# Three of the eight pieces of six modulation parts computed on GpSimd instead of VectorE in a two-block transformer kernel

## The chip, the core and the metric

The kernel runs on one core of one Trainium2 chip. The core has engines with a queue each: TensorE (PE in the profile; its weight loads are PEld), VectorE (DVE), ScalarE (ACT), GpSimd (POOL) and SyncE (SP), which here only issues DMAs. Every queue is worked through in order, so an instruction that waits holds up all that stand behind it on its engine. The time is the device time of one launch in microseconds. Before the change it was 1309.55 us (median of three runs, 1307.87 to 1313.42).

## What is computed

Two blocks of two layers each over 256 tokens of width 1024, all in float32. The change lies in the first block, in the vectors that scale, shift and gate each of its layers:

```python
cs = jax.nn.silu(c)
for layer in range(DEPTH):
    mod = cs @ ada_w[layer] + ada_b[layer]
    shift, scale, gate = jnp.split(mod, 3, axis=-1)
    h = rms_norm(x, norm_g[layer]) * (1.0 + scale[:, None, :]) + shift[:, None, :]
    ...
    y = even_mixer(...)      # layer 0; odd_mixer(...) in layer 1
    x = x + gate[:, None, :] * y
```

`cs` is one row of 1024 numbers and `ada_w[layer]` is 1024 x 3072, so the product is a matrix times a vector: little arithmetic for many bytes (25 MB for both layers).

## The kernel before

**The modulation.** A layer's 3072 results are cut into three parts (0 shift, 1 scale, 2 gate) of two halves of 512 columns. For one half of a part the 1024 rows of weights come as eight pieces of 128 x 512 (`k` = 0 to 7), 256 KB each. VectorE multiplies piece `k` by the column `cs[:, k]` and sums the pieces in an accumulator `macc` (`add_k`, L457: a TENSOR_SCALAR for the first piece at L462, a SCALAR_TENSOR_TENSOR at L464 for the others). GpSimd adds the row of `ada_b` into the accumulator's first partition (L519). One matmul with a matrix of ones (L523) then sums over the partitions and spreads the result over all of them, and `finish` (L466) puts it where the layer reads it. Shift and scale of layer 0 are made at the start of the kernel by another function (`start`). The other eight halves are *later parts*: `part` (L511) starts one each time that the function `later` (L889) is called, and `later` first finishes the one before. They are numbered 0 to 7 here in the order of the list `todo`: gate of layer 0 (0, 1), scale of layer 1 (2, 3), shift of layer 1 (4, 5), gate of layer 1 (6, 7).

**What runs beside them.** The later parts are spread over the attention of layer 0 (`even_layer`). Its projections stream weights through `unit` (L220 to L230): SyncE loads `wr` (L224, three buffers), ScalarE rounds it to `wh` (L227), VectorE makes the remainder `wl` (L228; five buffers each), and TensorE does three products for each pair (L245 to L247). Attention of a first kind (heads `scores_a`, `values_a`) has its row minimum with bias on VectorE (L398), the exponential on ScalarE (L401), the scaling by the row's sum on VectorE (L678), then transposes on TensorE (L410); a second kind (`scores_b`, `values_b`) has L398, L401 and L731 in these places, and a GpSimd power (L337) before L751. The results are gated (L592, L579) and go through the output projection with the weights `ab_w_out`.

**What sets the order.** The pieces `aw` have three buffers, and their loads (L517) share SyncE's queue with the weight loads (L224) and the bias tables (L416). A framework schedules the program at build time: it interleaves the instructions of each engine by priorities and by its own estimate of times, and the result is a fixed order per engine. So a change in one place can give another order on all engines. The accumulators `macc` have two buffers.

## Time and profile before

| | |
|---|---|
| time, median of three runs | 1309.55 us |
| the profiled execution: time | 1304.1 us |
| the profiled execution: span of the trace | 1302.3 us |
| TensorE / VectorE / ScalarE / GpSimd busy | 95% / 65% / 49% / 5% of the span |
| the later parts' accumulation | 56.6 to 183.5 us of the span |

The page of the profile gives the busy time of each engine over the span. A view by stretches gives the same for chosen pieces of time; a view by lines groups the instructions by line and form and says what ended the idle time ahead of them; the view of waits says which engine waited for which instruction; the timeline lists instructions with start and length. On GpSimd and VectorE an instruction's length runs from its start to its end, so time in which it is held up after its start counts in its length. Neighbouring VectorE instructions overlap by a little: a SCALAR_TENSOR_TENSOR of 0.75 us starts 0.67 us after the one before.

### The profile page before, as it was taken

How to read it: one execution, taken by the hardware profiler on the slowest of the kernel's cores; microseconds unless marked ns; L12 is line 12 of the kernel's file. 1: busy time of each engine (PE TensorE's matmuls, PEld its weight loads, DVE VectorE, ACT ScalarE, POOL GpSimd, SP SyncE). 2: the span in 40 equal slices, each digit the busy share in tenths (PEclk: the TensorE clock that was granted, in tenths of full speed). 3: DMA queues.
4: the chain of work that ended last, by engine and by line, in shares of the span. 5: the costliest groups of instructions: out<-in, count | busy, mean ns of one | idle time of the engine just before them, and what ended most of it. 6: DMA issues, size and time to landing. Idle time of an engine off the chain costs nothing.

```text
span 1302.3 us, 21332 instructions
## 1 busy us (share of the span) xinstructions
PE 1240.6 (95%) x8352; PEld 1047.7 (80%) x8352; DVE 851.2 (65%) x1456; ACT 644.0 (49%) x1083; POOL 68.9 (5%) x82
## 2 busy tenths in 40 slices
PE   6889889999899999999999999999999999999997
PEld 3767667977787777887899987987787887999986
DVE  6977888676658755766755544668755757655543
ACT  3454645685655345444644433556345444544432
POOL 0021120000101000000000000010000000000000
PEclk8999999999999999999999999999999999999999
DMA  8988865654553233465666654753242564766552
GB/s 315 325 274 277 257 197 172 202 179 122 178 170 98 84 114 98 149 210 162 196 186 185 181 192 129 234 149 96 82 128 83 177 196 130 226 183 188 180 192 81
DMA packets 104960, 227.25 MB, mean 175 GB/s; under 512 B 8206, under 2 KB 8350, under 8 KB 104860
## 3 DMA queue, kind: packets, MB, share of 16 engines
q1 hardware_dynamic: 102560, 219.18, 54.0%
q0 software_dynamic: 1984, 6.60, 1.8%
q8 instruction: 65, 1.06, 0.3%
q14 instruction: 35, 0.29, 0.1%
q10 hardware_dynamic: 316, 0.12, 0.0%
HBM read 224.82 MB, written 1.05 MB: 173 GB/s over the span
## 4 chain that ended last, share of the span: by engine, by line
PE 70%; DVE 7%; issue 5%; ACT 3%; DMA 2%; POOL 1%; POOLq 0%; DVEq 0%; ACTq 0%; SPq 0%
PE mm L246 20%; PE mm L245 19%; PE mm L247 19%; PE p L369 2%; DVE wl L228 2%; PE hs L1156 1%; ACT wh L227 1%; PE sc L376 1%; PE px L1440 1%; PE tr L324 1%; DMA wr<-in_gu_dram 1%; PE pv L385 1%; PE cm L376 1%; PE pt L410 1%; PE pv L1002 1%
## 5 line engine op out<-in xcount | busy, mean ns | idle before, releaser
L228 DVE TENSOR_TENSOR wl<-wr,wh 128x1024 fp32r<-128x1024 f32 (+1 forms) x372 | 431.3, 1165 | 268.6 <-ACT wh L227 266.5
L227 ACT CAST wh<-wr 128x1024 fp32r<-128x1024 f32 (+1 forms) x372 | 369.7, 1002 | 396.7 <-PE mm L247 164.7
L245 PE MATMUL mm<-hh,wh 128*128 128x256 f32 x1168 | 332.1, 286 | 1.0 <-ACT hh L328 0.9
L247 PE MATMUL mm<-hh,wl 128*128 128x256 f32 x1168 | 332.7, 285 | 0.0
L246 PE MATMUL mm<-hl,wh 128*128 128x256 f32 x1168 | 332.3, 285 | 0.0
L245 PEld LDWEIGHTS mm<-hh,wh 128*128 128x128 f32 x1168 | 224.4, 193 | 3.7 <-ACT hh L328 1.9
L247 PEld LDWEIGHTS mm<-hh,wl 128*128 128x128 f32 x1168 | 224.5, 192 | 2.1 <-issue 1.9
L246 PEld LDWEIGHTS mm<-hl,wh 128*128 128x128 f32 x1168 | 224.6, 192 | 1.5 <-issue 1.2
L246 PE MATMUL mm<-wl,hh 128*128 128x512 f32 (+1 forms) x448 | 178.3, 398 | 1.5 <-DVE wl L228 1.5
L245 PE MATMUL mm<-wh,hh 128*128 128x512 f32 (+1 forms) x448 | 177.3, 396 | 0.9 <-DVE ropet L1069 0.4
L247 PE MATMUL mm<-wh,hl 128*128 128x512 f32 (+1 forms) x448 | 175.5, 392 | 0.4 <-DVE hl L329 0.3
L246 PEld LDWEIGHTS mm<-wl,hh 128*128 128x128 f32 x448 | 85.0, 190 | 19.7 <-DVE wl L228 2.4
L245 PEld LDWEIGHTS mm<-wh,hh 128*128 128x128 f32 x448 | 84.9, 190 | 18.7 <-ACT hh L328 1.2
L247 PEld LDWEIGHTS mm<-wh,hl 128*128 128x128 f32 x448 | 84.8, 189 | 17.0 <-DVE hl L329 1.4
L245 PE MATMUL mm<-wh,ff 128*128 128x512 f32 x176 | 69.5, 395 | 0.0
L246 PE MATMUL mm<-wl,ff 128*128 128x512 f32 x176 | 69.5, 395 | 0.0
L247 PE MATMUL mm<-wh,ff 128*128 128x512 f32 x176 | 69.4, 395 | 0.0
L464 DVE SCALAR_TENSOR_TENSOR macc<-aw,cs,macc 128x512 f32<-128x512 f32 x78 | 58.4, 762 | 11.9 <-DMA aw<-in_ada_w_dram 11.5
L401 ACT ACTIVATE p<-p,nm 128x256 f32<-128x256 f32 (+1 forms) x80 | 39.7, 497 | 32.0 <-DVE nm L398 29.2
L246 PE MATMUL mm<-wl,yTh 128*128 128x512 f32 x128 | 50.6, 396 | 1.1 <-DVE wl L228 1.1
L247 PE MATMUL mm<-wh,yTl 128*128 128x512 f32 x128 | 50.0, 390 | 0.0
L245 PE MATMUL mm<-wh,yTh 128*128 128x512 f32 x128 | 49.4, 395 | 0.1
(388 smaller groups left out, 1533.7 us busy)
## 6 DMA issues: line engine op xcount, KB each, us to landing
wr<-in_w_in_dram SPq DMA_DIRECT2D x120, 512.0 KB, 3.8
wr<-in_gu_dram SPq DMA_DIRECT2D x88, 512.0 KB, 3.7
wr<-in_w_ffn_down_dram SPq DMA_DIRECT2D x44, 512.0 KB, 3.3
aw<-in_ada_w_dram SPq DMA_DIRECT2D x80, 256.0 KB, 3.9
wr<-in_ab_w_in_dram SPq DMA_DIRECT2D x32, 512.0 KB, 5.3
wr<-in_c_w_in_dram SPq DMA_DIRECT2D x20, 512.0 KB, 4.4
wr<-in_w_branch_dram SPq DMA_DIRECT2D x16, 512.0 KB, 3.2
wr<-in_w_out_dram SPq DMA_DIRECT2D x16, 512.0 KB, 3.2
```

Source lines behind the costliest of these rows:

```text
L227: nc.scalar.copy(hi[:, i:i + m], raw[:, i:i + m])
L228: nc.vector.tensor_sub(lo[:, i:i + m], raw[:, i:i + m], hi[:, i:i + m].bitcast(F32))
L245: mm(out, lhsT=ah, rhs=bh, start=start, stop=False, **kw)
L246: mm(out, lhsT=ah, rhs=bl, start=False, stop=False, **kw)
L247: mm(out, lhsT=al, rhs=bh, start=False, stop=stop, **kw)
L324: nc.tensor.transpose(ps[:, j * 128:(j + 1) * 128], src[:, (g + j) * 128:(g + j + 1) * 128], self.ident)
L369: self.nc.tensor.matmul(out[r], lhsT=lhsT[:, r], rhs=rhs, **kw)
L376: mm = lambda out, lhsT, rhs: self.nc.tensor.matmul(out, lhsT=lhsT, rhs=rhs, start=True, stop=True)
L385: mm = lambda hh, kc: self.nc.tensor.matmul(ps[HALF[hh], :], lhsT=vs(hh, kc), rhs=pTs[hh][:, kc * 256:kc * 256 + 256], start=(kc == 0), st ...
L401: nc.scalar.activation(p, p, AF.Exp, bias=nm, scale=-1.0, accum_out=l)
L410: nc.tensor.transpose(ps[:, kc * 256 + t * 128:kc * 256 + t * 128 + 128], p[:, t, kc * 128:kc * 128 + 128], self.ident)
L464: nc.vector.scalar_tensor_tensor(acc, w, n.cs[:, k:k + 1], acc, op0=OP.mult, op1=OP.add)
```

## The change

```diff
     def part(self, part, half):
         n, nc = self.n, self.n.nc
         acc = n.s2("macc", tag="macc")
-        for k in range(8):
-            w = n.s2("aw", tag="aw")
-            nc.sync.dma_start(w, self.src(part, half, k, 1))
-            self.add_k(acc, k, w, k == 0)
-        nc.gpsimd.tensor_add(acc[0:1, :], acc[0:1, :], self.row(part, half))
+        if self.l == 0 or part != 2:
+
+            acc2 = n.s2("macc2", tag="macc")
+            for k in (0, 1, 3, 2, 4, 6, 5, 7):
+                w = n.s2("aw", tag="aw")
+                nc.sync.dma_start(w, self.src(part, half, k, 1))
+                if k in (0, 3, 6):
+                    nc.gpsimd.tensor_scalar(w if k else acc2, w, n.cs[:, k:k + 1], None, op0=OP.mult)
+                    if k:
+                        nc.gpsimd.tensor_add(acc2, acc2, w)
+                else:
+                    self.add_k(acc, k, w, k == 1)
+            nc.gpsimd.tensor_add(acc2[0:1, :], acc2[0:1, :], self.row(part, half))
+            nc.gpsimd.tensor_add(acc, acc, acc2)
+        else:
+            for k in range(8):
+                w = n.s2("aw", tag="aw")
+                nc.sync.dma_start(w, self.src(part, half, k, 1))
+                self.add_k(acc, k, w, k == 0)
+            nc.gpsimd.tensor_add(acc[0:1, :], acc[0:1, :], self.row(part, half))
...
-    with n.phase(mod=(4, D), aw=(3, 512), macc=(2, 512), bias=(3, 512), p=(4, 512), pT=(2, 512), yp=(8, 256),
+    with n.phase(mod=(4, D), aw=(3, 512), macc=(3, 512), bias=(3, 512), p=(4, 512), pT=(2, 512), yp=(8, 256),
                  s2=(12, 512)):
```

In the six later parts 0 to 5, pieces 0, 3 and 6 go to GpSimd: each is multiplied by its column there, and the second and third are added into an accumulator of their own, `macc2`. The row of `ada_b` goes into `macc2`, and GpSimd adds `macc2` to VectorE's sum of the other five pieces. Parts 6 and 7 stay as they were. The accumulators have three buffers instead of two. Line numbers behind `part` grow by 15.

GpSimd's queue at part 2 (`macc_944` before, `macc_952` and `macc2_953` now; `lv`, `G1` and `sub` are small loads that GpSimd issues). Before:

```order
L167 DMA lv_1488<-in_rows_dram 128x64 [waits DMAHW7_49,DMAHW3_49,Pool_49]
L167 DMA lv_1488<-in_rows_dram 128x64 x3
L167 DMA G1_940<-in_rows_dram 128x1024
L167 DMA sub_1498<-in_rows_dram 128x128 [waits DMASW5_49,DMASW4_49,DMASW6_49,DMASW3_49,DVE_49]
L519 TENSOR_TENSOR macc_944<-macc_944,adab_969 1x512 [waits DMAHW5_49,DVE_49,PE_49]
```

Now:

```order
L522 TENSOR_SCALAR macc2_953<-aw_954,cs_123 128x512 [waits DMAHW6_49,Pool_49]
L167 DMA G1_948<-in_rows_dram 128x1024
L522 TENSOR_SCALAR aw_960<-aw_960,cs_123 128x512 [waits DMAHW5_49,DMAHW3_49,DMAHW0_49]
L524 TENSOR_TENSOR macc2_953<-macc2_953,aw_960 128x512 [waits Pool_49]
L522 TENSOR_SCALAR aw_970<-aw_970,cs_123 128x512 [waits DMAHW4_49,DMAHW0_49,DVE_49]
L524 TENSOR_TENSOR macc2_953<-macc2_953,aw_970 128x512 [waits Pool_49]
L527 TENSOR_TENSOR macc2_953<-macc2_953,adab_980 1x512 [waits Pool_49]
L167 DMA sub_1514<-in_rows_dram 128x128 [waits Pool_49]
L528 TENSOR_TENSOR macc_952<-macc_952,macc2_953 128x512 [waits DVE_49,PE_49]
```

One instruction of GpSimd has become seven, six of them over 128 partitions, and the load of `sub` stands behind six of them.

VectorE's queue at part 3 (`macc_1000` before, `macc_1012` now), beside the projection that follows the first attention. Before:

```order
L464 SCALAR_TENSOR_TENSOR macc_1000<-aw_1007,cs_123,macc_1000 128x512 [waits DMAHW2_49,DVE_49]
L464 SCALAR_TENSOR_TENSOR macc_1000<-aw_1010,cs_123,macc_1000 128x512 [waits DMAHW4_49,DVE_49]
L228 TENSOR_TENSOR wl_1290<-wr_1288,wh_1289 128x1024 [waits DMAHW7_49,PE_49,Activation_49]
L464 SCALAR_TENSOR_TENSOR macc_1000<-aw_1013,cs_123,macc_1000 128x512 [waits DMAHW5_49,DVE_49]
L464 SCALAR_TENSOR_TENSOR macc_1000<-aw_1016,cs_123,macc_1000 128x512 [waits DMAHW7_49,DVE_49]
L228 TENSOR_TENSOR wl_1296<-wr_1294,wh_1295 128x1024 [waits DMAHW1_49,PE_49,Activation_49]
```

Now:

```order
L464 SCALAR_TENSOR_TENSOR macc_1012<-aw_1024,cs_123,macc_1012 128x512 [waits DMAHW3_49,DVE_49]
L228 TENSOR_TENSOR wl_1300<-wr_1298,wh_1299 128x1024 [waits PE_49,Activation_49]
L464 SCALAR_TENSOR_TENSOR macc_1012<-aw_1027,cs_123,macc_1012 128x512 [waits DMAHW4_49,DVE_49]
L228 TENSOR_TENSOR wl_1306<-wr_1304,wh_1305 128x1024 [waits DMAHW1_49,PE_49,Activation_49]
L464 SCALAR_TENSOR_TENSOR macc_1012<-aw_1034,cs_123,macc_1012 128x512 [waits DMAHW7_49,DVE_49]
```

Between two `wl` there is now one piece where there were two.

VectorE's queue where the last weights of `ab_w_in` are split (the last `wl` of that matrix is `wl_1844` before, `wl_1868` now; `macc_2878` and `macc_2902` are part 6, `macc_2976` and `macc_3000` part 7). Before:

```order
L464 SCALAR_TENSOR_TENSOR macc_2976<-aw_2989,cs_123,macc_2976 128x512 [waits DMAHW7_49,DVE_49]
L335 TENSOR_SCALAR var_1816<-ss_1809 128x2 [waits Activation_49]
L228 TENSOR_TENSOR wl_1844<-wr_1842,wh_1843 128x1024
L751 SCALAR_TENSOR_TENSOR yb_1808<-pv_1807,rstd_1818,sub_1498 128x128 [waits Pool_49]
L751 SCALAR_TENSOR_TENSOR yb_1808<-pv_1807,rstd_1818,sub_1498 128x128
```

Now:

```order
L464 SCALAR_TENSOR_TENSOR macc_2902<-aw_2924,cs_123,macc_2902 128x512 [waits DMAHW7_49,DVE_49]
L228 TENSOR_TENSOR wl_1868<-wr_1866,wh_1867 128x1024 [waits PE_49]
L739 RECIPROCAL rl_1782<-l_1785 128x1 [waits Activation_49]
L398 ISA p_1781,nm_1783<-sc_1764,bias_1761 128x256
L398 ISA nm_1783 128x1
```

The last `wl` has moved from the middle of part 7 to the end of part 6.

## Rows read from the trace of the kernel before

**Rows 1.** The page: span, and busy time of each engine.

```profile
span 1302.3 us, 21332 instructions
PE 1240.6 (95%) x8352; PEld 1047.7 (80%) x8352; DVE 851.2 (65%) x1456; ACT 644.0 (49%) x1083; POOL 68.9 (5%) x82
```

**Rows 2.** Stretches: length, then busy us (instructions) per engine, clock, DMA share, GB/s.

```profile
56.00:160.00 104.00, 89.67 (x564) 72.26 (x562) 83.69 (x195) 54.01 (x120) 18.10 (x18) 0.95 0.87 281
90.00:105.00 15.00, 9.49 (x65) 7.12 (x62) 8.90 (x31) 6.72 (x18) 1.17 (x3) 0.96 0.83 264
105.00:125.00 20.00, 20.00 (x150) 17.70 (x150) 15.80 (x22) 9.09 (x13) 2.60 (x3) 0.95 0.86 269
160.00:196.00 36.00, 32.00 (x160) 24.99 (x159) 31.75 (x69) 17.91 (x41) 8.05 (x8) 1.00 0.67 205
310.00:1302.00 992.00, 968.27 (x6725) 832.59 (x6723) 607.10 (x891) 476.00 (x707) 35.02 (x39) 1.00 0.51 155
```

**Rows 3.** Lines with forms, VectorE, 56 to 196 us: busy us, mean ns | idle before.

```profile
L464 DVE SCALAR_TENSOR_TENSOR macc<-aw,cs,macc 128x512 f32<-128x512 f32 x56 | 43.0, 768 | 11.0 <-DMA aw<-in_ada_w_dram 10.9
L228 DVE TENSOR_TENSOR wl<-wr,wh 128x1024 fp32r<-128x1024 f32 x28 | 34.1, 1220 | 3.9 <-ACT wh L227 3.6 <-issue 0.3
```

**Rows 4.** Waits, 47-215 us (`wl`: 170-185, SyncE: 40-200): us in total, times, longest.

```profile
PE pt L410 <- DVE p L731: 6.1, 3, 3.4
PE pt L410 <- DVE p L678: 5.7, 4, 2.8
...
PE mm L246 <- DVE wl L228: 1.6, 2, 1.2
...
SPq L517 <- DVE macc L464: 17.9, 29, 1.4
```

**Rows 5.** Timeline, VectorE and GpSimd: the row adds L519 and their neighbours; start, us.

```profile
39.44 6.05 DVE L464 SCALAR_TENSOR_TENSOR macc<-aw,cs,macc 128x512 f32<-128x512 f32 x9
...
72.42 1.51 POOL L519 TENSOR_TENSOR macc<-macc,adab 1x512 f32<-1x512 f32 x1 [5.96 <-DVE rl L668]
72.71 1.38 DVE L678 TENSOR_SCALAR p<-p,rl 128x256 f32<-128x256 f32 x1
...
94.60 0.35 DVE L678 TENSOR_SCALAR p<-p,rl 128x256 f32<-128x256 f32 x1
...
124.38 2.15 POOL L519 TENSOR_TENSOR macc<-macc,adab 1x512 f32<-1x512 f32 x1 [14.65 <-DVE macc L464]
125.30 0.42 DVE L398 CUSTOM_DVE_ANT_0 p<-sc,bias 128x256 f32<-128x256 f32 x1
125.72 1.36 DVE L464 SCALAR_TENSOR_TENSOR macc<-aw,cs,macc 128x512 f32<-128x512 f32 x1
...
138.73 2.15 POOL L519 TENSOR_TENSOR macc<-macc,adab 1x512 f32<-1x512 f32 x1 [12.20 <-PE mm L247]
...
183.59 1.27 POOL L519 TENSOR_TENSOR macc<-macc,adab 1x512 f32<-1x512 f32 x1 [2.44 <-issue]
183.97 2.47 DVE L579 TENSOR_TENSOR yb<-yb,sg 128x128 f32<-128x128 f32 x8
```

**Rows 6.** Timeline, GpSimd's other work on tiles, and VectorE beside the first.

```profile
57.08 2.14 DVE L464 SCALAR_TENSOR_TENSOR macc<-aw,cs,macc 128x512 f32<-128x512 f32 x2
57.75 0.92 POOL L194 CAST msk<-mskf 128x896 uint8<-128x896 f32 x1 [4.00 <-DMA mskf<-in_msk_dram]
...
390.54 0.61 POOL L1402 COPY Y<-cst 128x512 f32<-128x512 f32 x1 [2.16 <-DVE shift L1323]
401.85 2.75 POOL L1402 COPY Y<-cst 128x512 f32<-128x512 f32 x1 [10.71 <-DVE ar L1373]
```

**Rows 7.** The chain that ended last, 182 to 191 us: start, us, what.

```profile
182.79 0.66 DVE macc L464
...
184.94 1.49 DVE yb L579 x7
...
188.90 2.28 DVE wl L228 x2
```

## The prediction

> **What bounds the kernel now.** I read the page first, then the stretches, and from there only the stretch that the change touches. TensorE is busy 95% of the span, VectorE 65%, GpSimd 5% [rows 1]: on the page, VectorE looks like an engine with room and GpSimd like one that is free. The stretches say where that average comes from. Behind 310 us TensorE is busy 968 of 992 us and nothing of the change runs there [rows 2]. Parts 0 to 5 lie between 56 and 160 us. There TensorE is busy 89.7 of 104 us, VectorE 83.7, and the DMA engines 87% [rows 2]: three resources near their limit, none at it, each waiting for the others in turn. TensorE's own waits in and just behind that stretch are mostly for VectorE's scaled rows: 6.1 + 5.7 = 11.8 us in seven waits before the transposes [rows 4]. So an earlier VectorE is worth something here, and a later one costs. From 160 to 196 us VectorE is busy 31.8 of 36 us [rows 2], and the chain that ended last runs through its accumulation and its `wl` to the output weights [rows 7]; parts 6 and 7 lie there, and they are not changed. The largest single item of VectorE in 56 to 196 us is L464, 56 instructions and 43.0 us [rows 3], so the change does aim at the right line.
>
> **What is removed.** Six parts lose three SCALAR_TENSOR_TENSOR each, 18 in all; each part keeps one TENSOR_SCALAR. Back to back, nine of them took 6.05 us, 0.67 us each; the mean length is 0.77 us [rows 3, 5]. At 0.70 us the 18 are 12.6 us of VectorE.
>
> **What is added.** Each of the six parts has on GpSimd three TENSOR_SCALAR of 128x512, two TENSOR_TENSOR that sum them and one that joins the two accumulators; the row add was there before. The two-input add with 512 elements per partition takes 1.27 us when nothing holds it, as at 183.59 us [rows 5]; there it works on one partition, and I take the same for 128, since the elements per partition are the same. The multiplication by a column is not in the trace. From below the nearest row is the copy of 128x512, 0.61 us, from above the add, 1.27 us [rows 5, 6]. I take 0.65, near the copy, since both read one tile and write one. A part is 3 x 0.65 + 3 x 1.27 = 5.8 us, six parts 34.6 us (34 to 46 by the two ends). With the 18.1 us that it has now, GpSimd is busy some 53 of 104 us [rows 2]: it has the time and does not become the bound by its sum.
>
> The Trainium skill ("GPSIMD Engine Reference", section "Performance versus the Vector engine") gives 769 ns as measured for 512 elements in its best loop. By that estimate the added work would be 36.7 us, 2.1 more; no run here shows it.
>
> **What GpSimd's work costs VectorE.** This is the term that decides, and the row adds show it. When the add at 72.42 us runs, the scaling that starts at 72.71 takes 1.38 us instead of 0.35: 1.03 lost. At 125.72 a SCALAR_TENSOR_TENSOR takes 1.36 instead of 0.75: 0.61 lost; that add itself started at 124.38 but took 2.15 us, 0.88 more than the undisturbed one, since VectorE was in the middle of a `wl`; the row minimum at 125.30, which reads PSUM and one tile, took its usual 0.42. At 183.97 eight gatings take 2.47 us of which the last seven are 1.49, so the first took 0.97 for 0.21: 0.76 lost. Beside the add at 138.73 nothing is lost, because VectorE was waiting for ScalarE anyway [rows 5, 7]. There are eight adds; read in the same way they cost VectorE between 0 and 1.05 us each and 0.76 on average, 60% of the 1.27. It is not special to adds: the one-input cast at 57.75 stretches a pair of L464 to 2.14 us where two take 1.4 [rows 6]. And the wait goes the other way as well: the copy at 401.85 took 2.75 us instead of 0.61 while VectorE ran two-input instructions without a gap [rows 6]. So the two engines take turns whenever VectorE reads two tiles or scales one, which is most of what it does here.
>
> With 60% of 34.6 us VectorE loses 20.7 us and saves 12.6: **8.1 us more** in the stretch, not less. Bounds: nothing lost (as at 138.73), 12.6 us less; all of GpSimd's added time lost, 22 us more. I take the 60% because it is a mean of eight adds in this very stretch, and keep both ends.
>
> The Trainium skill ("SBUF — State Buffer", section "Who interferes with whom") says that GpSimd and a VectorE instruction with two SBUF inputs share a read interface, that the first to start keeps it for its whole instruction, and that the other blocks entirely. The trace agrees that one blocks the other (1.36 us for 0.75), but VectorE then loses 60% of an add and not all of it, since it is sometimes idle or in an instruction that does not need the interface. By the bare rule the loss is the upper end, 22 us net: it is rival B below.
>
> **How much reaches the end.** Part 3 lies where TensorE is busy 20.0 of 20 us (105 to 125): a later VectorE costs nothing there as long as the split weights stay ahead. Part 2 lies where VectorE is busy 8.9 of 15 us (90 to 105): half. The other four count in full. That is 4.5 of 6 parts, 8.1 x 0.75 = 6.1 us. Against it stands the new order near the end: the last `wl` of `ab_w_in` comes before part 7 and no longer in its middle, where TensorE waited 1.6 us for `wl` in two waits [rows 4]. I count these 1.6 us as gained: 6.1 - 1.6 = **4.5 us longer**.
>
> **Edits costed at nothing.** The row of `ada_b` and the joining add come at the end of a part, and its matmul with the ones is only asked for by the next `later`, some 15 us on: if GpSimd is late by more than that, TensorE waits in order. The load of `sub`, behind six GpSimd instructions of part 2, is followed on VectorE by an instruction that needs it; TensorE's full stretch covers a few microseconds there. The powers of L337 stand behind part 5's work; VectorE waits for them already. The buffers are a wash by my count: VectorE now waits for 18 landings fewer (it lost 10.9 us on 56 pieces, so some 3 us), but pieces 3 and 6 of a part are held for a multiplication and an add, 1.9 us instead of 0.75, twelve times, on three buffers (14 us / 3 = 4.6 us of buffer time), and SyncE already waits 17.9 us for such buffers [rows 3, 4].
>
> **Rivals.**
>
> A, *the turns fall into VectorE's gaps* (faster). VectorE idles 20.3 of 104 us [rows 2], and a multiplication that starts when its piece lands may meet exactly the gap in which VectorE used to wait for that piece. For it: the add at 138.73 cost nothing. Against: seven of eight adds cost 0.6 us or more. It decides once the loss is under 12.6 / 34.6 = 36% of GpSimd's time. At 10%, 3.5 us, VectorE gains 9.1; three quarters of it and the 1.6 make 8.4 us, **1301**.
>
> B, *every turn costs its whole length* (slower). 22 us net on VectorE, 16.5 of it reaching the end, less 1.6: 14.9 us, **1324.5**. It decides from a loss of about 70%. For it: VectorE's queue in this stretch is full of two-tile instructions. Against: the measured 60%, and the full stretch of TensorE.
>
> C, *the piece buffers hold SyncE* (slower). SyncE issues in order, so a piece that waits for GpSimd holds up the weights behind it. If the 14 us of longer holding, with GpSimd's own waiting for its turn (0.9 us each as at 124.38, 11 us), reach the end at a quarter, 6 us come on top: **1320**. Against: the split weights have five buffers, so TensorE has work while SyncE waits, as from 105 to 125 us [rows 2].
>
> D, *nothing shows*: TensorE's prefetch covers it all, **1309.5**.
>
> **How the numbers follow.** The sum is made on the profiled execution, 1304.1 us with 1.8 us around its span; it lies 5.4 us under the median of the three runs. A changed kernel profiled alike should show about 1308.6; the timed median I put at 1309.55 + 4.5 = **1314.0 us**. A measurement of this kernel tells about 0.5%, 6.5 us, from no change: 1303.0 to 1316.1 is "the same". Chances: forecast 42% (34 within the bound, 8 above), A 26% (22 under it, 4 within), B 16% and C 11% above, D 5% within. Faster 22%, same 43%, slower 35%. The range from 1300 to 1324 leaves out half of A's far end and of B's.
>
> **What would show it.** Right: VectorE's L464 falls to 60 instructions over the kernel, GpSimd's busy time rises by 35 to 45 us, and VectorE's other two-tile lines in 56 to 160 us grow in mean length, so that its busy time there does not fall by 12.6 us but stays or rises; the stretch from 56 to 196 us is 3 to 6 us longer. A: the mean lengths hardly change and the waits of L410 for VectorE shrink. B: L228 shows a mean well over 1.4 us. C: SyncE's waits for GpSimd, and TensorE waiting for `wl`. What would make it wrong altogether is a multiplication on GpSimd that takes far more than 1.27 us.

## The result, and the profile after

The changed kernel takes 1326.9 us (median of four runs, 1325.4 to 1327.8) against 1308.7 us before (1307.5 to 1313.4): a ratio of 1.0142, 95% interval 1.0120 to 1.0164. It is 18 us slower. The prediction was 1314.0 us with a range from 1300 to 1324: its sum pointed the right way, with 4.5 us where 18 came.

The page of the changed kernel, to be held against [rows 1]:

```profile
span 1324.5 us, 21355 instructions
PE 1248.3 (94%) x8352; PEld 1052.5 (79%) x8352; DVE 847.4 (64%) x1438; ACT 644.8 (49%) x1083; POOL 125.0 (9%) x118
```

VectorE has its 18 instructions fewer and is busy 3.8 us less, where the prediction had 8.1 us more. GpSimd is busy 56.1 us more, where the prediction had 34.6. The loss lies ahead of 247 us. The view by stretches, first of the kernel before, then of the changed one (columns as in [rows 2]); the cut is where TensorE has done the same 1027 instructions:

```profile
0.00:225.00 225.00, 189.16 (x1027) 146.19 (x1028) 183.32 (x382) 107.64 (x222) 31.26 (x38) 0.95 0.80 261
225.00:1302.00 1077.00, 1051.44 (x7326) 901.52 (x7324) 667.87 (x1075) 536.39 (x861) 37.68 (x44) 1.00 0.51 157
```

```profile
56.00:160.00 104.00, 81.31 (x490) 64.93 (x488) 69.82 (x150) 46.26 (x100) 65.54 (x49) 0.89 0.77 248
0.00:247.00 247.00, 197.59 (x1027) 150.96 (x1028) 180.81 (x364) 108.63 (x223) 87.31 (x74) 0.91 0.72 238
247.00:1324.00 1077.00, 1050.75 (x7327) 901.49 (x7325) 666.59 (x1074) 536.18 (x861) 37.66 (x44) 1.00 0.49 156
```

The later stretch is the same to a microsecond: 1077 us with 1051 us of TensorE. The early one is 22 us longer (this is one execution against one; the medians differ by 18). Of the 22, TensorE idles 13.6 us more (49.4 against 35.8), and 8.4 us are the same instructions at a lower granted clock, 0.91 of full speed instead of 0.95 in the mean, which in this trace goes with an engine that waits more often. VectorE is busy *less* there. So this is a loss by waiting, and the sum of VectorE's own work does not account for it. Between 56 and 160 us, where VectorE was busy 83.7 us with 195 instructions [rows 2], it is busy 69.8 with 150: its work comes later.

GpSimd's added work, by lines from 0 to 215 us (busy us, mean ns, then idle before):

```profile
L522 POOL TENSOR_SCALAR aw<-aw,cs 128x512 f32<-128x512 f32 x12 | 19.3, 1605 | 31.3 <-DMA aw<-in_ada_w_dram 11.5 <-DVE nm L398 7.1 <-DVE p L693 6.7
L524 POOL TENSOR_TENSOR macc<-macc,aw 128x512 f32<-128x512 f32 x12 | 17.3, 1444 | 0.9
L522 POOL TENSOR_SCALAR macc<-aw,cs 128x512 f32<-128x512 f32 x6 | 11.0, 1830 | 36.0 <-DMA aw<-in_ada_w_dram 35.8
L528 POOL TENSOR_TENSOR macc<-macc,macc 128x512 f32<-128x512 f32 x6 | 9.2, 1530 | 3.9 <-DVE macc L464 3.8
```

These are 56.8 us. The multiplication by a column takes 1.56 us when nothing holds it (the shortest of the 18 is 1.55), more than the add with 1.26, and far more than the 0.65 that the prediction took from a copy.

Waits of the changed kernel, 47 to 215 us (us in total, times, longest), those that [rows 4] has no row for:

```profile
SPq L520 <- POOL macc L524: 30.6, 10, 6.2
SPq L520 <- POOL macc L522: 14.7, 5, 4.5
...
ACT ka L623 <- POOL macc L527: 10.4, 1, 10.4
ACT p L401 <- POOL macc L527: 4.6, 1, 4.6
...
DVE macc L462 <- POOL macc L528: 5.4, 1, 5.4
...
PE pt L410 <- DVE p L746: 7.7, 2, 7.3
PE sc L376 <- ACT ka L623: 7.1, 1, 7.1
```

Three in-order queues now wait for GpSimd: SyncE with the next pieces (45.3 us), ScalarE with `ka` behind the load of a row of `ada_b` whose buffer GpSimd's row add still holds (10.4 us), and VectorE with a new accumulator (5.4 us). The last of these, in the timeline of GpSimd and then VectorE:

```profile
129.80 1.61 POOL L527 TENSOR_TENSOR macc<-macc,adab 1x512 f32<-1x512 f32 x1
132.85 1.56 POOL L522 TENSOR_SCALAR macc<-aw,cs 128x512 f32<-128x512 f32 x1 [1.44 <-DMA aw<-in_ada_w_dram]
134.38 1.26 POOL L528 TENSOR_TENSOR macc<-macc,macc 128x512 f32<-128x512 f32 x1
...
129.37 0.90 DVE L464 SCALAR_TENSOR_TENSOR macc<-aw,cs,macc 128x512 f32<-128x512 f32 x1 [0.80 <-DMA aw<-in_ada_w_dram]
135.68 0.49 DVE L462 TENSOR_SCALAR macc<-aw,cs 128x512 f32<-128x512 f32 x1 [5.40 <-POOL macc L528]
```

The joining add L528 of part 3 stands in GpSimd's queue behind the first multiplication of part 4, which waits for its piece to land. VectorE's first instruction of part 4 needs the accumulator that this add frees, and behind it in VectorE's queue stand the row minima of the second attention. TensorE's longest wait, 7.3 us before the transposes at 150.71, is for the first scaled rows of that attention. Those rows were held once more at the end, by the joining add of part 4:

```profile
148.49 1.89 POOL L528 TENSOR_TENSOR macc<-macc,macc 128x512 f32<-128x512 f32 x1
149.18 2.31 DVE L746 SCALAR_TENSOR_TENSOR p<-p,rl 128x256 f32<-128x256 f32 x2
```

Two such scalings take 0.87 us in the kernel before (at 133.83 us), so 1.4 of the 7.3 us are a turn of GpSimd's. The wait costs TensorE its clock too, by the view of stretches:

```profile
137.00:143.00 6.00, 6.00 (x29) 4.95 (x27) 4.69 (x8) 0.60 (x2) 3.05 (x2) 1.00 0.72 238
...
150.00:154.00 4.00, 3.29 (x10) 2.47 (x11) 3.52 (x10) 1.67 (x5) 1.99 (x2) 0.50 0.77 239
```

Between them TensorE is busy 0.4 of 7 us. Behind this pause the granted clock is 0.50, 1.2 of 2.4 GHz, where it was 1.00 ahead of it. But this longest wait is not by itself the loss: five_pieces, the first experiment below, has nearly the same one and is no slower than the kernel before.

### The profile page after: what moved, and what is told of

Read it like the earlier page. It is cut to its first block, busy times and chain, and to the rows that moved or that the text cites. A ratio compares the mean times of both kernels' runs of the same rounds, so it can differ in the third digit from the quotient of the medians.

```text
span 1324.5 us, 21355 instructions
## 1 busy us (share of the span) xinstructions
PE 1248.3 (94%) x8352; PEld 1052.5 (79%) x8352; DVE 847.4 (64%) x1438; ACT 644.8 (49%) x1083; POOL 125.0 (9%) x118
## 3 DMA queue, kind: packets, MB, share of 16 engines
q1 hardware_dynamic: 102560, 219.18, 50.9%
## 4 chain that ended last, share of the span: by engine, by line
PE 70%; DVE 10%; issue 7%; DMA 6%; ACT 3%; POOL 3%; SPq 0%; POOLq 0%; DVEq 0%; ACTq 0%
PE mm L246 19%; PE mm L245 19%; PE mm L247 19%; DMA aw<-in_ada_w_dram 4%; DVE wl L228 2%; PE p L369 2%; PE sc L376 2%; ACT wh L227 1%; PE hs L1171 1%; DVE macc L464 1%; DMA wr<-in_gu_dram 1%; POOL aw L522 1%; PE px L1455 1%; PE pv L385 1%; PE cm L376 1%
## 5 line engine op out<-in xcount | busy, mean ns | idle before, releaser
L228 DVE TENSOR_TENSOR wl<-wr,wh 128x1024 fp32r<-128x1024 f32 (+1 forms) x372 | 436.9, 1181 | 278.4 <-ACT wh L227 277.7
L246 PE MATMUL mm<-hl,wh 128*128 128x256 f32 x1168 | 334.9, 287 | 0.0
L246 PEld LDWEIGHTS mm<-hl,wh 128*128 128x128 f32 x1168 | 226.3, 194 | 2.1 <-issue 1.8
L246 PE MATMUL mm<-wl,hh 128*128 128x512 f32 (+1 forms) x448 | 178.3, 398 | 0.5 <-DVE wl L228 0.4
L246 PEld LDWEIGHTS mm<-wl,hh 128*128 128x128 f32 x448 | 84.7, 189 | 18.6 <-issue 1.7
L246 PE MATMUL mm<-wl,ff 128*128 128x512 f32 x176 | 69.6, 395 | 0.0
L353 POOL TENSOR_TENSOR rstd<-var,mhalf 128x1 f32<-128x1 f32 x12 | 9.0, 748 | 602.2 <-DVE var L352 602.2
L464 DVE SCALAR_TENSOR_TENSOR macc<-aw,cs,macc 128x512 f32<-128x512 f32 x60 | 46.5, 791 | 17.0 <-DMA aw<-in_ada_w_dram 16.7
L246 PE MATMUL mm<-wl,yTh 128*128 128x512 f32 x128 | 50.4, 395 | 1.3 <-DVE wl L228 1.3
```

What stands on the lines that cost most here:

```text
L228: nc.vector.tensor_sub(lo[:, i:i + m], raw[:, i:i + m], hi[:, i:i + m].bitcast(F32))
L246: mm(out, lhsT=ah, rhs=bl, start=False, stop=False, **kw)
L464: nc.vector.scalar_tensor_tensor(acc, w, n.cs[:, k:k + 1], acc, op0=OP.mult, op1=OP.add)
```

## The experiments

Five theories were on the table: *turns* (VectorE and GpSimd hold each other up, called port theory in the expectations), *ring* (pieces that GpSimd holds stop SyncE's loads), *row* (the load of `ada_b`'s row in ScalarE's queue; one expectation calls ring and row together the holding theory), *coupling* (any of these queues, each taking over when another is cut), and *order* (another order costs by itself). A change of order cannot be kept out of these kernels: the framework moves some instructions on every engine after nearly any edit.

All runs in one table. "Ratio" is against the kernel before on the same chip. "Reads" is the time of GpSimd's instructions that read tiles (TENSOR_TENSOR, TENSOR_SCALAR, COPY, CAST), 0 to 240 us. "VectorE waits" are its waits for accumulators that GpSimd holds and for the small loads that GpSimd issues (`lv`, `sub`, `sk`), 40 to 235 us. "TensorE waits" is the sum of the rows of its view of waits, 47 to 235 us.

| kernel | ratio, 95% interval | reads, us | VectorE waits, us | TensorE waits, us |
|---|---|---|---|---|
| before | 1 | 23 | 1.9 | 23.4 |
| five_loads | 0.9949, 0.9932–0.9965 | 23 | 5.1 | 21.2 |
| writes_only | 0.9994, 0.9976–1.0011 | 21 | 0.0 | 22.6 |
| join_only | 1.0002, 0.9986–1.0019 | 31 | 1.0 | 21.7 |
| before_macc3 | 1.0002, 0.9990–1.0015 | 22 | 1.4 | 23.1 |
| five_pieces | 1.0014, 0.9995–1.0032 | 22 | 4.9 | 27.6 |
| before_rows | 1.0019, 1.0004–1.0035 | 24 | 2.0 | 24.1 |
| writes_long | 1.0041, 1.0021–1.0060 | 19 | 1.5 | 26.1 |
| before_five_buffers | 1.0051, 1.0033–1.0069 | 21 | 3.7 | 24.9 |
| paced_reads | 1.0061, 1.0044–1.0078 | 78 | 6.2 | 31.0 |
| free_gpsimd | 1.0084, 1.0064–1.0104 | 89 | 6.3 | 30.6 |
| one_piece | 1.0092, 1.0077–1.0107 | 45 | 11.3 | 38.4 |
| one_piece_rows | 1.0100, 1.0072–1.0128 | 42 | 12.6 | 35.6 |
| rows_gpsimd | 1.0135, 1.0101–1.0168 | 79 | 8.8 | 33.7 |
| after | 1.0142, 1.0120–1.0164 | 79 | 7.8 | 35.8 |
| own_row | 1.0149, 1.0119–1.0179 | 80 | 0.0 | 34.2 |
| own_buffers | 1.0202, 1.0187–1.0217 | 77 | 17.2 | 41.8 |
| own_queue_rows | 1.0213, 1.0175–1.0251 | 84 | 23.7 | 42.2 |
| resident_source | 1.0233, 1.0213–1.0253 | 78 | 20.2 | 37.1 |
| own_queue | 1.0265, 1.0237–1.0293 | 85 | 24.1 | 50.9 |

### What VectorE's 18 instructions were worth

```diff
                 if k in (0, 3, 6):
-                    nc.gpsimd.tensor_scalar(w if k else acc2, w, n.cs[:, k:k + 1], None, op0=OP.mult)
-                    if k:
-                        nc.gpsimd.tensor_add(acc2, acc2, w)
+                    pass
...
-            nc.gpsimd.tensor_add(acc2[0:1, :], acc2[0:1, :], self.row(part, half))
-            nc.gpsimd.tensor_add(acc, acc, acc2)
+            nc.gpsimd.tensor_add(acc[0:1, :], acc[0:1, :], self.row(part, half))
```

> The changed kernel with GpSimd's share of the sum left out: pieces 0, 3 and 6 of the six parts are loaded and thrown away, so the modulation lacks three eighths of its sum (six parts); the row of ada_b goes into VectorE's accumulator as before. It shows what VectorE's 18 fewer instructions are worth when GpSimd costs nothing. Ring theory (pieces that GpSimd holds stop SyncE's loads), row theory (the load of ada_b's row, which waits for GpSimd's row add, blocks ScalarE's queue) and port theory (VectorE and GpSimd take turns) all expect the loss gone: 1295 to 1307 us, against 1309 before and 1327 after. Order theory (another order of the program costs the 18 us, whatever GpSimd does): it stays above 1318.

Measured 1308.2 us, 1.0014. The work is gone from VectorE and nothing has come in its place, and the time is the same as before: the change had nothing to gain that could be measured. It is not a pure price of the 18 instructions, since the order differs as well. In this order VectorE waits 4.9 us for `sk`, and the row of TensorE's longest wait is

```profile
PE pt L410 <- DVE p L742: 7.1, 1, 7.1
```

where the kernel before has 3.4 [rows 4], so a gain of a few us could be hidden. VectorE's lines of this run, 47 to 230 us, beside which the changed kernel's are read below:

```profile
L228 DVE TENSOR_TENSOR wl<-wr,wh 128x1024 fp32r<-128x1024 f32 x38 | 46.2, 1220 | 12.9 <-ACT wh L227 12.8
L464 DVE SCALAR_TENSOR_TENSOR macc<-aw,cs,macc 128x512 f32<-128x512 f32 x38 | 28.3, 746 | 16.3 <-DMA aw<-in_ada_w_dram 16.2
L689 DVE TENSOR_SCALAR p<-p,rl 128x256 f32<-128x256 f32 x16 | 6.6, 430 | 0.0
```

L464 went from 43.0 us [rows 3] to 28.3, and its waits for pieces from 10.9 to 16.2, those of L228 for ScalarE from 8.9 to 12.8 in the same stretch: what VectorE no longer computes it waits. The next kernel asks whether transfers are what it waits for:

```diff
-            for k in (0, 1, 3, 2, 4, 6, 5, 7):
+            for k in (1, 2, 4, 5, 7):
```

> The kernel of five_pieces without the loads of the pieces that it throws away: 18 transfers of 256 KB fewer, 4.7 MB. If transfers bound this stretch (some 270 GB/s before), up to 17 us go: 1291 to 1300, and that is why 18 instructions less on VectorE gained nothing. If VectorE or the order of the work bounds it, it stays at 1304 to 1310.

Measured 1300.3 us, 0.9949: by the ratios some 8 us less than five_pieces for 4.7 MB fewer, at the edge of the first range. So transfers look like a part of the bound, and only a part: 4.7 MB at the 281 GB/s of [rows 2] would be 17 us.

### Cutting one queue at a time

GpSimd multiplies a tile that is there already, and nobody waits for its reading the pieces:

```diff
-                    nc.gpsimd.tensor_scalar(w if k else acc2, w, n.cs[:, k:k + 1], None, op0=OP.mult)
+                    p = n.csB[:, 512:1024] if k else acc2
+                    nc.gpsimd.tensor_scalar(p, n.csB[:, 0:512], n.cs[:, k:k + 1], None, op0=OP.mult)
                     if k:
-                        nc.gpsimd.tensor_add(acc2, acc2, w)
+                        nc.gpsimd.tensor_add(acc2, acc2, p)
```

> The changed kernel with GpSimd's three multiplications per part reading a tile that is already in SBUF (csB) and writing another, instead of reading and writing the piece: the same instructions of the same length on GpSimd, but no piece waits for them, and they wait for no piece. The modulation is wrong in three eighths of its sum. Port theory: stays at 1322 to 1330, since GpSimd still takes 57 us of turns. Ring theory: the pieces come free on landing, 1308 to 1314. Row theory: in the order that this gives, the load of the row stands well ahead of GpSimd's need, so 1308 to 1314 too.

Measured 1335.9 us, 1.0233: worse than the change itself. SyncE no longer waits for GpSimd at all (49.0 us in the changed kernel, with a piece of part 6) and ScalarE 3.2 us (15.0), so the ring and the row are out as the only cause. The row of its waits (40 to 230 us) that stands out:

```profile
DVE macc L462 <- POOL macc L529: 10.2, 2, 6.3
```

Then buffers of their own for GpSimd's pieces:

```diff
-                w = n.s2("aw", tag="aw")
+                if k in (0, 3, 6):
+                    n.ng_i = 1 - getattr(n, "ng_i", 0)
+                    w = n.csB[:, n.ng_i * 512:n.ng_i * 512 + 512]
+                else:
+                    w = n.s2("aw", tag="aw")
```

> The changed kernel with two buffers of their own for GpSimd's pieces (the halves of csB, which is idle by then), so that VectorE's five pieces have the three aw buffers to themselves; everything is computed. Ring theory: GpSimd's 1.56 + 1.27 us a piece no longer hold the loads of VectorE's pieces and the weights behind them; SyncE's 45 us of waiting for GpSimd fall under 20 and the time to 1309 to 1315. Row theory: the 10.4 us that ScalarE's ka waits behind the load of the row stay, 1320 to 1327. Port theory: no change, 1324 to 1328.

Measured 1331.1 us, 1.0202, outside what any of the three expected. SyncE still waits for GpSimd's pieces, since it issues all loads in order (34.3 us), and VectorE waits for the accumulator 12.9 us:

```profile
DVE macc L462 <- POOL macc L532: 12.9, 2, 7.3
```

Then buffers of its own for the row of `ada_b`:

```diff
-    def row(self, part, half):
+    def row(self, part, half, own=False):
+        if own:
+            bb = self.n.csB[:, half * 512:half * 512 + 512]
+        else:
             bb = self.n.par("adab")
...
```

> The changed kernel with two buffers of their own for the row of ada_b (halves of csB) instead of the par pool's three, so that its load has nothing to wait for when ScalarE's queue comes to it; the pieces stay on the three aw buffers. Row theory: ScalarE's 10.4 and 4.6 us of waiting for GpSimd's row add go, and with them 8 to 15 us: 1312 to 1319. Ring theory: 1320 to 1327, the waits of SyncE stay. Port theory: no change, 1324 to 1328.

Measured 1324.2 us, 1.0149. ScalarE's waits for the row add fell only from 15.0 to 10.4 us, so this cut was half a cut. But its order also put the loads of `sub` and `sk` at the start of the kernel (GpSimd issues them at 34.4 and 38.1 us): VectorE waits for neither of them, nor for an accumulator, and the loss is the same as with the change. A whole cut of the row loads the rows of all eight parts through GpSimd's queue:

```diff
-    def row(self, part, half):
+    def row(self, part, half, q=None):
...
-        self.n.nc.scalar.dma_start(bb[0:1, :], bass.AP(tensor=r.tensor, offset=o, ap=[[1, 1], [1, 512]]))
+        (q or self.n.nc.scalar).dma_start(bb[0:1, :], bass.AP(tensor=r.tensor, offset=o, ap=[[1, 1], [1, 512]]))
...
-            nc.gpsimd.tensor_add(acc2[0:1, :], acc2[0:1, :], self.row(part, half))
+            nc.gpsimd.tensor_add(acc2[0:1, :], acc2[0:1, :], self.row(part, half, nc.gpsimd))
...
```

> The changed kernel with one edit: the rows of ada_b of all eight later parts are loaded through GpSimd's own DMA queue, so no load in ScalarE's in-order queue waits for a buffer that GpSimd's row add holds. own_row had only halved that wait (6.7 and 3.7 us were left), and in own_queue the same load, for part 6, held ScalarE for 19.5 us. Row theory: all of ScalarE's waits for GpSimd go, 1314 to 1319. Port theory alone: 1323 to 1328. Ring theory: 1320 to 1326, SyncE's waits for the pieces stay.

Measured 1324.1 us, 1.0135. ScalarE no longer waits for GpSimd at all, and the time is the same as with the change: 10.4 us in the view of waits, the longest single one on ScalarE, were worth nothing that can be measured.

### Cutting all of them

GpSimd loads its own three pieces and the row, into its own buffers, and sums into its own accumulator:

```diff
                 if k in (0, 3, 6):
+                    n.ng_i = 1 - getattr(n, "ng_i", 0)
+                    w = n.csB[:, n.ng_i * 512:n.ng_i * 512 + 512]
+                    nc.gpsimd.dma_start(w, self.src(part, half, k, 1))
...
```

> The changed kernel, everything computed, with GpSimd cut off from the other queues: it issues the loads of its own three pieces a part and of the row of ada_b itself, into two buffers of its own, and sums into an accumulator of its own (macc has two buffers again). Only the joining add is left between the engines. Coupling theory: 1306 to 1313. Port theory: 1320 to 1332, the instructions on GpSimd are the same.

Measured 1340.6 us, the slowest of all. Its waits, 40 to 230 us:

```profile
ACT kb L628 <- POOL macc L532: 19.5, 1, 19.5
...
DVE sk L847 <- issue: 13.0, 1, 13.0
...
DVE sub L729 <- issue: 11.1, 1, 11.1
...
PE sc L376 <- ACT kb L628: 20.0, 1, 20.0
```

The 20 us are the row of part 6, which was still loaded from ScalarE's queue and waited for a buffer that GpSimd's row add held. With that mended:

> own_queue with the rows of parts 6 and 7 loaded through GpSimd's queue as well, so that nothing but the joining add is left between GpSimd and the other queues. own_queue lost 20.0 us where TensorE waited for kb behind such a row. Port and coupling together (10 us of turns, as free_gpsimd shows against five_pieces, and the rest waiting): 1315 to 1322. Coupling alone: 1307 to 1312. Port alone as the whole loss: 1325 to 1332.

Measured 1334.7 us, 1.0213, again above the range of any theory. What is left are VectorE's 12.9 and 10.8 us for `sk` and `sub`, two small loads that GpSimd issues and that now stand in its queue behind its own loads and sums. This fits the coupling theory in that a cut queue is replaced by another. Cutting all of them at the pieces was not enough: GpSimd's queue also serves others.

### Reading and holding apart

Here nobody waits for GpSimd's sums (they are thrown away, pieces 0, 3 and 6 too, and VectorE adds the row):

```diff
...
-            nc.gpsimd.tensor_add(acc, acc, acc2)
+            nc.gpsimd.tensor_add(acc2, acc2, n.csB[:, 0:512])
+            nc.vector.tensor_add(acc[0:1, :], acc[0:1, :], self.row(part, half))
```

> GpSimd does the same eighteen multiplications and as many adds, but bound to nothing: it multiplies a tile that is already in SBUF, sums into a tile that nobody reads, and VectorE's sum of five pieces goes to the matmul without GpSimd (the row of ada_b is added on VectorE). Pieces 0, 3 and 6 are loaded and thrown away, so the modulation lacks three eighths of its sum. Port theory: the turns remain, so 1320 to 1332. Coupling theory (in every variant some in-order queue, SyncE by the pieces, ScalarE by the row, VectorE by the accumulators, waits for a late GpSimd, and with it the loads): 1306 to 1312, near five_pieces with 1308.

Measured 1318.1 us, 1.0084, between the two. But GpSimd, bound to nothing, was busy 40 of the first 56 us. So the same with each part's work begun when the part's first piece for VectorE lands:

```diff
...
+                    if k == 1:
+                        nc.gpsimd.tensor_copy(n.csB[:, 0:1], w[:, 0:1])
+                        for i in (0, 3, 6):
...
```

> free_gpsimd, but each part's work on GpSimd begins when that part's first piece for VectorE has landed, so that the reads lie where the changed kernel has them (56 to 160 us); still nobody waits for GpSimd's sums, pieces 0, 3 and 6 are loaded and thrown away. Port theory, direct: 1318 to 1328. If turns cost only with the waits that pass them on: 1308 to 1314.

Measured 1314.5 us, 1.0061: just above the second range, and by the ratios 6 us above five_pieces. That is what GpSimd's reading goes with when nobody waits for its sums, but no more than another order alone can make (see the controls). VectorE's L228 takes 1360 ns in the mean here, nearly as in the changed kernel (1386).

The other side is a GpSimd that writes to the pieces, accumulators and rows for as long as in the change but reads nothing except the row:

```diff
-                    nc.gpsimd.tensor_scalar(w if k else acc2, w, n.cs[:, k:k + 1], None, op0=OP.mult)
-                    if k:
-                        nc.gpsimd.tensor_add(acc2, acc2, w)
+                    if k:
+                        for _ in range(6):
+                            nc.gpsimd.memset(w, 0.0)
+                    else:
+                        nc.gpsimd.memset(acc2, 0.0)
+                        for _ in range(2):
+                            nc.gpsimd.memset(w, 0.0)
...
-            nc.gpsimd.tensor_add(acc, acc, acc2)
+            for _ in range(3):
+                nc.gpsimd.memset(acc, 0.0)
```

This is writes_long; writes_only has two writes in the place of each instruction, not three.

> The changed kernel with GpSimd's multiplications and adds replaced by writes of a constant over the same tiles, two for each, so that it holds the pieces, the accumulators and the rows as before but reads nothing; the modulation of the six parts is wrong altogether. If only reads make VectorE wait, L228 goes back to a mean near 1.22 us, and what is left is coupling: port and coupling together expect 1314 to 1320, coupling alone 1322 to 1328, port alone 1306 to 1311. If writes hold VectorE as well (L228 at 1.35 us and more), it tells them apart no further.

> writes_only with more writes: three in the place of each multiplication and each add (3 x 0.54 = 1.6 us against 1.56 and 1.27), so that GpSimd is busy and holds the pieces at least as long as in the changed kernel, and still reads nothing but the row. The modulation of the six parts is wrong altogether. Holding theory (the waits of SyncE and ScalarE for a late GpSimd make the loss): 1318 to 1327. Port theory (reading makes it): 1304 to 1311.

Measured 1305.5 us (0.9994) and 1310.2 us (1.0041). GpSimd is busy as long as in the change (58 us of writes in writes_long), and most of the loss is gone. But the waits did not come with the writes: SyncE waits 12.0 us for GpSimd in writes_long where it waited 49.0 with the change, ScalarE not at all where it waited 15.0, VectorE 1.5 where it waited 7.8. VectorE's L228 of writes_long, 47 to 230 us:

```profile
L228 DVE TENSOR_TENSOR wl<-wr,wh 128x1024 fp32r<-128x1024 f32 x36 | 45.1, 1256 | 15.8 <-ACT wh L227 15.8
```

1256 ns, against 1386 in the changed kernel and 1220 with no GpSimd work. So a GpSimd that writes leaves VectorE's two-tile instructions nearly alone, and being busy for as long costs about 5 us. What it costs that others wait for GpSimd is not measured by this run, since they wait so much less.

### How the loss grows with GpSimd's share

```diff
-                if k in (0, 3, 6):
+                if k == 0:
```

> The changed kernel with piece 0 alone on GpSimd, seven on VectorE; everything computed. Per part GpSimd has a multiplication, the row and the joining add, 2.8 us more than before where the change has 8.5. If the loss goes with GpSimd's reading time, a third of 18 us: 1312 to 1316. If it comes from the joining of the two sums and the order, it stays above 1320; if only the two pieces that are held for an add hurt, 1307 to 1310.

Measured 1317.7 us, 1.0092: 12 us for one piece where three cost 18. It does not go with the reading time. Two kernels ask what of it does it. join_only has no piece on GpSimd, only the second accumulator, its row and the joining add:

```diff
-                if k in (0, 3, 6):
+                if k == 8:
...
+            nc.gpsimd.memset(acc2, 0.0)
```

> The changed kernel with all eight pieces on VectorE, but with the second accumulator (set to zero by GpSimd), the row added to it and the joining add on GpSimd, and the three macc buffers; everything computed. If the loss of one_piece (12 us for one piece) comes from the joining add, which comes after VectorE's last piece, and from what waits for it: 1313 to 1318. If it comes from the multiplication that reads a piece: 1306 to 1310.

> one_piece with the rows of ada_b loaded through GpSimd's queue. Row theory: ScalarE's 10.6 us of waiting for GpSimd's row add were most of the 12 us: 1308 to 1311. If reading makes it, they lie beside other work, as in rows_gpsimd (1324 against 1327): 1314 to 1318.

join_only: 1306.5 us, 1.0002, no loss that can be measured. one_piece_rows: 1319.9 us, 1.0100, so the row's queue is not it either. What is left is the multiplication, by its reading, its length, or the order that comes with it. One place in one_piece_rows, in the timeline of GpSimd, then of VectorE:

```profile
129.25 2.19 POOL L528 TENSOR_TENSOR macc<-macc,macc 128x512 f32<-128x512 f32 x1 [9.33 <-DVE macc L464]
131.44 1.56 POOL L522 TENSOR_SCALAR macc<-aw,cs 128x512 f32<-128x512 f32 x1
133.08 1.60 POOL L527 TENSOR_TENSOR macc<-macc,adab 1x512 f32<-1x512 f32 x1
134.97 0.62 POOL L167 DMA_DIRECT2D sk<-in_rows_dram  x1 [0.29 <-POOL macc L527]
...
133.45 1.78 DVE L464 SCALAR_TENSOR_TENSOR macc<-aw,cs,macc 128x512 f32<-128x512 f32 x1
140.99 0.17 DVE L842 TENSOR_SCALAR sk<-sk 128x16 f32<-128x16 f32 x1 [5.76 <-DMA sk<-in_rows_dram]
```

VectorE idles from 135.2 to 141.0 for a table of 128 x 16 that GpSimd issued only at 134.97, behind a join that waited 9.33 us for VectorE, a multiplication and a row add. (The multiplication did not wait for its piece here.) In join_only the load stands behind the same join, a write and the row add, goes out at 129.52, and VectorE waits 1.0 us for it. Behind `sk` stand the row minima of the second attention, and TensorE does nothing at all from 140 to 150 us. Its row in the view of waits, 56 to 180 us (the last number is the longest):

```profile
PE pt L410 <- DVE p L746: 14.2, 2, 12.1
```

The same wait before the transposes of the second attention is 12.1 us in own_queue_rows too, where VectorE waited 12.9 us for `sk`, 3.4 us in the kernel before [rows 4], and 7.1 us in five_pieces, which is no slower.

### Controls on the kernel before

Three edits of the kernel before, without any of the change: two more buffers for pieces (the halves of `csB`, for pieces 1 and 4), the rows through GpSimd's queue, and three accumulators.

```diff
+            if k in (1, 4) and (self.l == 0 or part != 2):
+                w = n.csB[:, (k == 4) * 512:(k == 4) * 512 + 512]
```

> The kernel before with two more buffers for the pieces of the six parts (the halves of csB, for pieces 1 and 4). If SyncE's waits for piece buffers (some 50 us of waits in 40 to 230 us) hold up transfers that bound the stretch, 3 to 8 us faster, 1298 to 1302; if the weights' buffers take over the wait, no difference, 1303 to 1308.

```diff
-        nc.gpsimd.tensor_add(acc[0:1, :], acc[0:1, :], self.row(part, half))
+        nc.gpsimd.tensor_add(acc[0:1, :], acc[0:1, :], self.row(part, half, nc.gpsimd))
...
```

> The kernel before with the rows of ada_b of its eight later parts loaded through GpSimd's queue. Row theory: ScalarE's waits of 2.7 us for the row add and of 7.3 us for VectorE's last piece behind such a load go, 2 to 6 us faster, 1301 to 1306, and it beats both kernels. If those waits lie beside other work, no difference, 1306 to 1310; if another order costs by itself, up to 1314, like before_five_buffers.

```diff
-    with n.phase(mod=(4, D), aw=(3, 512), macc=(2, 512), bias=(3, 512), p=(4, 512), pT=(2, 512), yp=(8, 256),
+    with n.phase(mod=(4, D), aw=(3, 512), macc=(3, 512), bias=(3, 512), p=(4, 512), pT=(2, 512), yp=(8, 256),
```

> The kernel before with three macc buffers instead of two, which moves a few instructions on TensorE, VectorE, ScalarE and SyncE and nothing on GpSimd. No theory expects a difference by the work: 1305 to 1308. A time outside that is the size of what order alone can do here.

Measured 1313.6 us (1.0051), 1309.1 us (1.0019) and 1307.2 us (1.0002). None beats the kernel before. The first is a warning on the method: more buffers, VectorE's waits for pieces at L464 down from 10.9 to 3.3 us, and 7 us slower. An edit that reorders the program can move the time by 0.5%, and differences of that size between the kernels above are not evidence of a mechanism.

## Why the prediction was wrong, point by point

**The step that failed** is the way from VectorE's busy time to the end: "4.5 of 6 parts" of VectorE's net. VectorE's net came out as a small gain (12.6 us saved, about 11 lost), and the kernel became 18 us slower all the same, by TensorE's idling (13.6 us more between the profiles) and its lower clock (8.4 us). What the sum had no term for are the waits of three other queues for a late GpSimd, which the prediction put at nothing (SyncE 49.0 us, ScalarE 15.0, VectorE 7.8, between 40 and 235 us). The points follow its own order.

**What bounds the kernel.** The prediction saw three resources near their limit between 56 and 160 us and concluded that an earlier VectorE was worth something there. five_pieces says that it is worth nothing that can be measured. TensorE's waits for VectorE's scaled rows (11.8 us in seven waits) were read as VectorE being too busy; with 14.7 us less of L464 they are still 9.6 us in five_pieces, all of TensorE's waits together rise from 23.4 to 27.6, and VectorE waits for its own inputs instead.

**What is removed: 12.6 us.** The size is right (L464 fell by 14.7 us with 18 instructions fewer). That 4.5 of 6 parts of it reach the end is what failed: as far as can be measured, none of it does. It was counted as a gain against the loss by turns, so that the sum came out small. The 1.6 us counted as gained from the new order are of the right kind (TensorE's waits for `wl` at L246 fall from 2.3 to 1.3 us, 47 to 215 us), and too small to matter.

**What is added: 34.6 us.** Measured 56.8. The multiplication was taken at 0.65 us, "near the copy, since both read one tile and write one", with the add as its upper bound. It takes 1.56 us, above that bound: 18 x 0.91 = 16.4 us of the 22.2 too few, and the other 6 are GpSimd's own waiting (18 x 1.56 + 18 x 1.27 would be 51). A multiplication of far more than 1.27 us was what the prediction named as making it wrong altogether; this one is beyond the bound, and the term that it feeds, VectorE's loss, came out smaller all the same. The Trainium skill ("GPSIMD Engine Reference", section "Performance versus the Vector engine") has 769 ns for 512 elements in its best loop; the measurement decides, 1.26 us for the add and 1.56 us for the multiplication.

**What it costs VectorE: 20.7 us.** VectorE's lines of the changed kernel, 47 to 230 us, against those of five_pieces above:

```profile
L228 DVE TENSOR_TENSOR wl<-wr,wh 128x1024 fp32r<-128x1024 f32 x34 | 47.0, 1386 | 12.8 <-ACT wh L227 12.8
L464 DVE SCALAR_TENSOR_TENSOR macc<-aw,cs,macc 128x512 f32<-128x512 f32 x40 | 32.4, 813 | 16.0 <-DMA aw<-in_ada_w_dram 15.9
L693 DVE TENSOR_SCALAR p<-p,rl 128x256 f32<-128x256 f32 x16 | 7.7, 499 | 0.1
...
L746 DVE SCALAR_TENSOR_TENSOR p<-p,rl 128x256 f32<-128x256 f32 x8 | 5.0, 660 | 0.7 <-ACT p L745 0.6
```

34 x 0.166 = 5.6 us, 40 x 0.067 = 2.7, 16 x 0.069 = 1.1, and 8 x 0.183 = 1.5 for L746 (0.477 in five_pieces): some 11 us, half of the 20.7, from 56.8 us of GpSimd. The turns exist, but at a fifth of GpSimd's time and not at 60%, so VectorE's net is 12.6 saved against 11 lost. The 60% was the mean of eight adds, and the new work is half multiplications, which behave otherwise. Timeline of the changed kernel, two adds and two multiplications with the VectorE instruction beside each:

```profile
59.49 1.29 POOL L524 TENSOR_TENSOR macc<-macc,aw 128x512 f32<-128x512 f32 x1
59.59 1.47 DVE L462 TENSOR_SCALAR macc<-aw,cs 128x512 f32<-128x512 f32 x1
...
103.00 1.55 POOL L522 TENSOR_SCALAR aw<-aw,cs 128x512 f32<-128x512 f32 x1 [2.10 <-issue]
103.69 0.75 DVE L464 SCALAR_TENSOR_TENSOR macc<-aw,cs,macc 128x512 f32<-128x512 f32 x1 [2.90 <-DMA aw<-in_ada_w_dram]
...
109.05 1.56 POOL L522 TENSOR_SCALAR aw<-aw,cs 128x512 f32<-128x512 f32 x1 [3.14 <-DVE macc L464]
109.35 1.46 DVE L228 TENSOR_TENSOR wl<-wr,wh 128x1024 fp32r<-128x1024 f32 x1
110.70 1.30 POOL L524 TENSOR_TENSOR macc<-macc,aw 128x512 f32<-128x512 f32 x1
111.14 1.41 DVE L464 SCALAR_TENSOR_TENSOR macc<-aw,cs,macc 128x512 f32<-128x512 f32 x1
```

Beside the first add VectorE's scaling takes 1.47 us instead of 0.49, so it got going 1.08 us after the add's start; beside the second the L464 takes 1.41 instead of 0.75 and got going after 1.10 us. VectorE is kept out for most of the add. Beside the multiplication it is kept out for the beginning only. The L464 that starts 0.69 us into one takes its usual 0.75; the L228 that starts 0.30 us into one loses 0.24 (1.46 for 1.22), so it got going 0.54 us after the multiplication's start. The L228 at 58.15 and at 78.40 give the same 0.54, and each of the nine L464 and L228 that start 0.6 us or more into a multiplication takes its usual time. So the dearer instruction holds VectorE for less.

The Trainium skill ("SBUF — State Buffer", section "Who interferes with whom") says that a VectorE instruction with two SBUF inputs contends with a GpSimd instruction that reads SBUF and not with one that only writes, and the section has the other side blocked for a whole instruction. The runs nearly agree for the adds (1.08 and 1.10 us of 1.29 and 1.30) and agree for the writes (L228 at 1256 ns beside 58 us of writes). For the multiplication, which reads SBUF, the measurement differs: it blocks for its first 0.54 us of 1.56.

**Edits costed at nothing.** Here lie the terms that the sum lacked. The prediction named the load of `sub` behind six GpSimd instructions, the joining add, and the row, and waved each through: the add "is only asked for by the next `later`, some 15 us on", and TensorE's full stretch covers the load. TensorE's wait at that matmul is indeed small (2.7 us, ended by a VectorE instruction). But in the changed kernel VectorE's queue asks for the join's buffer earlier (L462, 5.4 us), ScalarE waits 15.0 us for row adds, and TensorE 7.1 us for `ka` behind one of them. `sub` costs VectorE 2.4 us there, against 1.9 before, and `sk`, which the prediction did not name, is not waited for; in other kernels both are, ahead of the second attention. Over the table VectorE's waits of this kind and TensorE's waits by and large rise together, up to 24.1 and 50.9 us in own_queue, where `sub` and `sk` make all of the 24.1. own_row is the exception: no such wait, L228 at 1236 ns, and a loss of 1.5%, there with 10.4 us of ScalarE waiting for GpSimd and 19.7 us of L228 waiting for ScalarE (12.8 in the changed kernel).

**The rivals.** A's condition came true, since 11 of 56.8 us is 19% and under its 36%, and its time of 1301 us did not: a gain of VectorE's does not reach the end. B had nearly the right time by luck (1324.5 for a measured 1326.9), with the wrong mechanism: VectorE was to lose 22 us net and is busy less than before. Its sign, L228 well over 1.4 us, did not come (1386 ns). Of C's signs SyncE's waits for GpSimd came (49.0 us) and TensorE's for `wl` did not (1.3 us, 2.3 before). The loss does not need them: resident_source and own_queue_rows have no such wait and are slower still. All of SyncE's waits between 40 and 230 us sum to 143 us before and 148 after: for the most part the name of the releaser has changed. D did not come; the interval of the ratio starts at 1.0120.

**What stays open.** Every kernel of the table with a multiplication on GpSimd loses 0.6% or more, and every kernel without one at most 0.5%. So the loss needs that work on GpSimd, and it arises as waiting; by which way is not shown. Reading that nobody waits for goes with 6 us over five_pieces in paced_reads and 9 in free_gpsimd, about what the edit of before_five_buffers moved without any of the change (7 us). What it costs that others wait for GpSimd was not measured apart. One piece already costs 12 us. That the rest goes through VectorE's in-order queue, behind GpSimd's late sums and small loads, fits the waits of the table and the timeline of one_piece_rows; own_row speaks against it as the only way, five_pieces has such waits at no loss, no run moved `sub` and `sk` alone to another queue, and the order of the program moved with every edit.

## What to carry to other kernels

Before moving work to a free engine, run the kernel with that work simply left out: if it is no faster, as here (1.0014), the move has little to gain. A busy share of 80% beside waits is no bound. When an in-order queue gets long work, list everything that already stands in it, small loads too, and who asks for each and when; in one kernel here VectorE awaited a 128 x 16 table for 6 us, within and ahead of 12 us in which TensorE stood still. Hold a long wait against a kernel that is no slower before calling it the loss: five_pieces has the longest one of the changed kernel too. And price an operation that the trace does not show wider than its neighbours: the bound above was the nearest row, and the truth lay outside it.

## What the runs showed of the hardware

On GpSimd a TENSOR_SCALAR of 128 x 512 with a column as operand takes 1.56 us, a TENSOR_TENSOR add of the same size 1.26 us, and a write of a constant 0.53 us. The multiplication by a column is the dearest of the three, although it reads one tile where the add reads two, and it kept VectorE's two-tile instructions out for 0.54 us where the add kept them out for 1.1 of its 1.3 us. Writes on GpSimd hold VectorE's scaling of the rows, a TENSOR_SCALAR of 128 x 256 in SBUF: 567 to 645 ns in the mean in the two kernels with writes, 430 in five_pieces, while L228 beside them hardly changed. And TensorE's granted clock took its share: 8.4 of the 22 us between the two profiles are the same instructions at a mean clock of 0.91 instead of 0.95. Behind the wait of 7.3 us the granted clock was 0.50 for the next 4 us, so that this wait cost more than its own length.
